# A feed-forward down projection by seven block products with tokens on partitions, in a two-layer fp32 trunk

## The chip, the cores and the metric

The kernel runs on one core of one Trainium2 chip. The metric is the time on the device of one execution, in microseconds (us); the median of several runs counts. The engines are TensorE (PE; its weight loads are PEld), VectorE (DVE), ScalarE (ACT), GpSimd (POOL) and SyncE (SP), which issues the DMA transfers of the kernel before.

## The reference

A trunk of two layers works on 512 tokens of 1024 features in float32. Layer 0 mixes the tokens with a gated recurrence (RG-LRU), layer 1 with stick-breaking attention over 16 heads. A root-mean-square norm stands ahead of each mixer and of each feed-forward part, and one at the very end. The feed-forward part, which the change is about, is

```python
def _swiglu(h, w_gate, w_up, w_down):
    g = h @ w_gate.astype(h.dtype)
    u = h @ w_up.astype(h.dtype)
    return (jax.nn.silu(g) * u) @ w_down.astype(h.dtype)
...
for each layer:
    x = x + mixer(_rmsnorm(x, g_mix))
    x = x + _swiglu(_rmsnorm(x, g_ffn), w_gate, w_up, w_down)
out = _rmsnorm(x, final_g)
```

with 2816 hidden features, so that `w_gate` and `w_up` are 1024 x 2816 and `w_down` is 2816 x 1024. (The last five lines are the reference's loop in short.)

## The kernel before

**Arithmetic.** Every large product is split to keep float32's accuracy: an operand is cast to fp32r on ACT (the high part, `wh` for weights, `hh`, `uh` for data), DVE or POOL subtracts that from the original (the low part `wl`, `hl`, `ul`), and PE runs high x high, high x low and low x high into one PSUM bank. One such triple is called mm3. Weights come as tiles of 128 x 1024, each loaded by one 512 KB transfer into a `raw` (or `b1`, `b3`) buffer. Such a tile is a *chunk*. `split_one` casts and subtracts it (L236, L237) two or three chunks ahead of its use.

**Layout.** The residual x is held transposed, as eight tiles `x0` to `x7` of 128 features x 512 tokens.

**Gate and up projections.** A feed-forward part runs in units u = 0 to 5 of 512 hidden features (256 for u = 5). Gate and up of a unit are computed by a one-level scheme of seven block products in place of eight (numbered 1, 5, 6, 3, 7, 2, 4), with tokens on partitions. Seven products need sums and differences of the blocks: those of the data are made once per layer (`ffn_in`), those of the weights per unit by DVE subtractions on 128 x 1024 tiles (`source`, L76), four per column of chunks, 88 in all. The results are combined into `r1`, `u2`, `b5`; SiLU is on ACT, and the products `u2` and `hx` are the hidden values with tokens on partitions.

**Down projection.** In unit u the hidden values of unit u-1 are transposed on PE (`turn`, L657, four banks), split into `hh` and `hl` (L660, L661), and multiplied by four chunks of `w_down` (`down_pair`): eight output tiles of 128 features x 512 tokens, each the sum of 4 k-tiles x 3 matmuls (L671 to L673), in the two banks `tb`; `add` (L676) adds each to its x. The last 256 features come after unit 5 in two chunks (`final`).

**The end.** In layer 0 each final add is followed by `norm_in`, which makes `uh` (L325), `ul` (L326) and the squares for attention's norm (L378, L380). In layer 1, `finish` scales x, transposes it on PE (L429), sums the squares on PE (L433), takes the root, and scales the rows out of PSUM (L454, L456) ahead of eight 256 KB stores (L457).

**Order.** Inside `ffn` only PE runs in the order of the program; DVE, ACT and POOL are ordered by a scheduler, with weight splits at high priority (`PRI`). All loads are on SP's queue; POOL does the low parts of the down chunks and additions of squares.

## Time and profile before

| what | value |
|---|---|
| median of 3 runs | 1148.85 us (1147.87 to 1149.36) |
| the profiled execution: its time | 1147.83 us |
| its span in the profile | 1146.0 us |
| feed-forward part, layer 0 / layer 1 | 166 to 512 / 785 to 1132 us |
| mean granted clock of PE | 0.995 |

The profile comes from one execution of its own; its span lies 1.8 us inside that execution's time. The busy time of an engine is read against the span; a wait is idle time of an engine ahead of an instruction, with the instruction that released it. Only what PE waits for, and what the end of the kernel takes, is on the way to the end. The windows view gives the same sums for a stretch; the timeline gives the start and the duration of single instructions, where a matmul's duration includes the depth of PE's pipeline, so that its price is the distance between starts.

### The profile page before, as it was taken

The numbers are of one execution on the slowest core, as the hardware profiler recorded it, in microseconds if no ns is written. First come the engines' busy times: TensorE is split into PE (matmuls) and PEld (weight loads), VectorE is DVE, ScalarE is ACT, GpSimd is POOL, SyncE is SP. The second block draws the span as 40 slices with busy tenths as digits, with TensorE's granted clock in tenths as the row PEclk, the third lists the DMA queues.
The fourth block names the chain that finished last, engine by engine and source line by source line (L and its number), as shares of the span: only waits on it lengthen the run. The fifth ranks groups of instructions, "written<-read, shape, count | busy, mean of one in ns | idle before, by whom it ended". The sixth has DMA issues, their size and how long they took to land.

```text
span 1146.0 us, 14365 instructions
## 1 busy us (share of the span) xinstructions
PE 1121.6 (98%) x5395; PEld 932.7 (81%) x5395; DVE 814.6 (71%) x1071; ACT 649.8 (57%) x969; POOL 295.1 (26%) x162
## 2 busy tenths in 40 slices
PE   9999999999999999999999999899999999999997
PEld 6887788788888888988888888778788888888896
DVE  7878889867574757473388888778967576675654
ACT  6598576634353444353489998767553534353443
POOL 2451333020111111262045345313011110211230
PEclk9999999999999999999999999999999999999999
DMA  7222234232423222122334234133433232322102
GB/s 244 89 90 89 98 105 171 95 110 76 142 74 129 73 92 92 55 92 92 111 97 125 82 86 110 37 99 122 147 110 110 73 114 80 121 86 99 58 35 74
DMA packets 36149, 114.23 MB, mean 100 GB/s; under 512 B 4592, under 2 KB 5616, under 8 KB 36080
## 3 DMA queue, kind: packets, MB, share of 16 engines
q1 hardware_dynamic: 36080, 113.32, 30.2%
q8 instruction: 42, 0.69, 0.2%
q14 instruction: 27, 0.22, 0.1%
HBM read 102.81 MB, written 2.10 MB: 92 GB/s over the span
## 4 chain that ended last, share of the span: by engine, by line
PE 74%; DVE 10%; ACT 4%; DMA 1%; issue 1%; POOL 0%; SPq 0%; DVEq 0%; POOLq 0%; ACTq 0%
PE bank L650 10%; PE bank L651 10%; PE bank L652 10%; PE bank L671 7%; PE bank L673 7%; PE bank L672 7%; PE bank L270 5%; PE bank L272 5%; PE bank L271 5%; DVE wl L237 4%; PE bank L974 3%; PE bank L657 2%; PE bank L1000 1%; DVE tt L76 1%; ACT wh L236 1%
## 5 line engine op out<-in xcount | busy, mean ns | idle before, releaser
L237 POOL TENSOR_TENSOR wl<-raw,wh 128x1024 fp32r<-128x1024 f32 (+1 forms) x74 | 178.5, 2412 | 641.9 <-ACT wh L236 638.0
L236 ACT CAST wh<-raw 128x1024 fp32r<-128x1024 f32 (+1 forms) x154 | 155.9, 1016 | 185.4 <-PE bank L652 88.1
L650 PE MATMUL bank<-wh,ow 128*128 128x512 f32 (+1 forms) x480 | 180.2, 375 | 3.8 <-DVE st L389 3.8
L651 PE MATMUL bank<-wl,ow 128*128 128x512 f32 (+1 forms) x480 | 178.9, 373 | 0.0
L652 PE MATMUL bank<-wh,ow 128*128 128x512 f32 (+1 forms) x480 | 178.8, 372 | 0.0
L236 ACT CAST wh<-tt 128x1024 fp32r<-128x1024 f32 x66 | 69.4, 1052 | 111.0 <-PE bank L672 55.1
L237 DVE TENSOR_TENSOR wl<-raw,wh 128x1024 fp32r<-128x1024 f32 (+1 forms) x80 | 97.9, 1227 | 45.4 <-ACT wh L236 44.4
L671 PE MATMUL bank<-hh,wh 128*128 128x512 f32 (+1 forms) x324 | 125.4, 387 | 0.0
L672 PE MATMUL bank<-hl,wh 128*128 128x512 f32 (+1 forms) x324 | 125.3, 387 | 0.0
L673 PE MATMUL bank<-hh,wl 128*128 128x512 f32 (+1 forms) x324 | 125.2, 387 | 0.0
L676 DVE TENSOR_TENSOR x<-x,bank 128x512 f32<-128x512 f32 x87 | 59.6, 685 | 85.1 <-PE bank L673 84.2
L650 PEld LDWEIGHTS bank<-wh,ow 128*128 128x128 f32 x480 | 90.8, 189 | 20.0 <-issue 2.7
L237 DVE TENSOR_TENSOR wl<-tt,wh 128x1024 fp32r<-128x1024 f32 x66 | 80.6, 1222 | 36.3 <-ACT wh L236 36.0
L270 PE MATMUL bank<-uh,wh 128*128 128x512 f32 x256 | 102.4, 400 | 1.7 <-ACT wh L236 1.1
L652 PEld LDWEIGHTS bank<-wh,ow 128*128 128x128 f32 x480 | 90.8, 189 | 15.8
L651 PEld LDWEIGHTS bank<-wl,ow 128*128 128x128 f32 x480 | 90.9, 189 | 15.4
L272 PE MATMUL bank<-uh,wl 128*128 128x512 f32 x256 | 100.2, 392 | 1.0 <-DVE wl L237 1.0
L271 PE MATMUL bank<-ul,wh 128*128 128x512 f32 x256 | 99.7, 390 | 0.3 <-DVE ul L326 0.3
L237 DVE TENSOR_TENSOR wl<-b,wh 128x1024 fp32r<-128x1024 f32 x44 | 54.8, 1246 | 51.8 <-ACT wh L236 51.6
L236 ACT CAST wh<-b 128x1024 fp32r<-128x1024 f32 x44 | 46.3, 1053 | 62.1 <-PE bank L652 26.7
L673 PEld LDWEIGHTS bank<-hh,wl 128*128 128x128 f32 x324 | 60.9, 188 | 12.4
L671 PEld LDWEIGHTS bank<-hh,wh 128*128 128x128 f32 x324 | 60.9, 188 | 12.1
(220 smaller groups left out, 2421.2 us busy)
## 6 DMA issues: line engine op xcount, KB each, us to landing
raw<-w_gu SPq DMA_DIRECT2D x44, 512.0 KB, 3.5
b<-w_gu SPq DMA_DIRECT2D x44, 512.0 KB, 4.0
raw<-w_dn SPq DMA_DIRECT2D x44, 512.0 KB, 3.5
raw<-w_qk SPq DMA_DIRECT2D x16, 512.0 KB, 3.5
raw<-w_in SPq DMA_DIRECT2D x14, 512.0 KB, 3.6
raw<-w_ao SPq DMA_DIRECT2D x8, 512.0 KB, 4.0
raw<-w_v SPq DMA_DIRECT2D x8, 512.0 KB, 3.5
qh<-qx SPq DMA_DIRECT2D x32, 128.0 KB, 2.4
```

What stands on the lines that cost most here:

```text
L236: self.nc.scalar.copy(wh[:, c], raw[:, c])
L237: self.wl_engine(i).tensor_tensor(wl[:, c], raw[:, c], wh[:, c].bitcast(F32), ALU.subtract)
L270: mm(out, lhsT=wh, rhs=xh, start=first, stop=False)
L271: mm(out, lhsT=wh, rhs=xl, start=False, stop=False)
L272: mm(out, lhsT=wl, rhs=xh, start=False, stop=last)
L650: mm(out[j][:, :w], lhsT=oh[:, ts(j)], rhs=wh[:, ws], start=st, stop=False, skip_group_check=True)
L651: mm(out[j][:, :w], lhsT=oh[:, ts(j)], rhs=wl[:, ws], start=False, stop=False, skip_group_check=True)
L652: mm(out[j][:, :w], lhsT=ol[:, ts(j)], rhs=wh[:, ws], start=False, stop=en, skip_group_check=True)
L671: mm(out, lhsT=w[0][:, ws], rhs=h[:, cs], start=st, stop=False, skip_group_check=True)
L672: mm(out, lhsT=w[0][:, ws], rhs=lw[:, cs], start=False, stop=False, skip_group_check=True)
L673: mm(out, lhsT=w[1][:, ws], rhs=h[:, cs], start=False, stop=en, skip_group_check=True)
L676: nc.vector.tensor_tensor(self.x[m], self.x[m], bank, ALU.add)
```

## The change

**Down projection.** The hidden values and `w_down` are now cut into 2 x 2 blocks as well. `dproduct` runs the seven block products d1 to d7 of a unit, 12 matmuls each, with *tokens on partitions*: results are added to `y`, four tiles of 128 tokens x 1024 features. The stationary operands are sums of transposed blocks of hidden values: t0 and t1 (`turn`) transpose the features 0, 2 and 1, 3 into the two banks `tb`, and `operands` makes the high and low parts `ha`, `hb`, `ht` from them (an ACT copy of one bank, four DVE sums of half tiles, then splits on ACT and DVE). t1 also copies `b5` out of the gate bank.

**Weight sums.** The sums of gate and up weights are made by *accumulating DMAs* on POOL's queue (`plus`): a piece of `w_gu` is added in memory to a buffer (`bu`, `bv`) that held an earlier piece, one chunk after the split that last read it (`soon`). In units 0, 1 and 5 ("direct") product 6's sum stays on DVE. There are 78 such transfers of 512 KB. The sums of `w_down` blocks are four POOL subtractions per unit (`DownPiece.after`), three of them behind d1's split. POOL also makes the low parts of the pieces d4, d5 and the second halves of products 2 and 7; DVE makes the others.

**x and y.** In layer 1, unit 0 transposes x into `y` (`turned`, steps x0 to x3, 32 transposes); in layer 0, y starts from the first block products, and at the end it is transposed back and added to x (`back`, 32 transposes). In layer 1 the last norm works on the rows of y (`finish`): per row tile two adds, two squares on ACT that also sum, a few 1-column operations, two scalings by the root and the gain, two stores.

**Order.** Inside `ffn`, ACT, DVE and POOL now stand in the order of the program as well. The steps of a unit are in strings (`order`). `plan` cuts the chunks in the same sequence. Splits run 4 chunks ahead and loads 9, x lies in the constant pool, slot pools have other sizes, `rsB` shares memory with `acc`.

The instructions change as follows: PE matmuls of 512 columns 4263 to 4161, of 256 columns 532 to 496, of 128 columns 408 to 440; DVE 1073 to 1245, ACT 971 to 1070, POOL 167 to 273.

Three places show how the program moves. First DVE in unit 3 of layer 0, around the down projection's operands. Before (`tt`, `b3`, `raw` are weight sums and their sources, `hl` the low hidden values, `wl` low weights):

```order
L237 TENSOR_TENSOR wl99_3124<-tt254_3121,wh99_3123 128x1024
L661 TENSOR_TENSOR hl0_96_3092<-bank6_76,hh0_96_3091 128x512
L661 TENSOR_TENSOR hl1_96_3100<-bank7_77,hh1_96_3099 128x512
L76 TENSOR_TENSOR tt254_3121<-b3_250_3037,tt254_3121 128x1024
L237 TENSOR_TENSOR wl101_3177<-tt253_3103,wh101_3176 128x1024
L661 TENSOR_TENSOR hl2_98_3148<-bank6_76,hh2_98_3147 128x512
L661 TENSOR_TENSOR hl3_98_3156<-bank7_77,hh3_98_3155 128x512
L76 TENSOR_TENSOR tt253_3103<-raw257_3231,tt253_3103 128x1024
```

After, from d1's split on (`t242` is the ACT copy in `operands`, `t243` and `t244` its sums):

```order
L295 TENSOR_TENSOR wl90_2803<-raw232_2662,wh90_2802 128x1024
L682 TENSOR_TENSOR t243_2832<-t242_2831,bank7_77 128x256
L681 TENSOR_TENSOR t244_2833<-t242_2831,bank6_76 128x256
L681 TENSOR_TENSOR t243_2832<-t243_2832,t242_2831 128x256
L681 TENSOR_TENSOR t244_2833<-bank7_77,t243_2832 128x256
L681 TENSOR_TENSOR hbl_1510<-bank7_77,hbh_1509 128x512
L681 TENSOR_TENSOR hal_1508<-t242_2831,hah_1507 128x256
L681 TENSOR_TENSOR htl_1512<-t243_2832,hth_1511 128x512
L681 TENSOR_TENSOR htl_1512<-t244_2833,hth_1511 128x512
L295 TENSOR_TENSOR wl91_2851<-bv_233_2683,wh91_2850 128x1024
L295 TENSOR_TENSOR wl492_2868<-bv_234_2702,wh492_2867 128x1024
L295 TENSOR_TENSOR wl93_2887<-raw235_2726,wh93_2886 128x1024
```

The weight sums are gone from DVE there; eight operations on hidden values stand in one block, and three splits follow them.

Second, POOL at the same place. Before, it holds only the low parts of down chunks:

```order
L237 TENSOR_TENSOR wl95_3016<-raw243_2873,wh95_3015 128x1024
L237 TENSOR_TENSOR wl4100_3160<-raw248_2995,wh4100_3159 128x1024
L237 TENSOR_TENSOR wl105_3266<-raw255_3127,wh105_3265 128x1024
L237 TENSOR_TENSOR wl4108_3334<-raw256_3199,wh4108_3333 128x1024
L237 TENSOR_TENSOR wl113_3446<-raw259_3305,wh113_3445 128x1024
```

After (`raw232` is block 11 of the unit's down weights, `raw235` block 21, `d12` and `d22` the other two, `dt` a sum of them):

```order
L152 TENSOR_TENSOR raw232_2662<-d12_236_2744,raw232_2662 128x1024
L152 TENSOR_TENSOR dt_241_2806<-d22_237_2746,raw232_2662 128x1024
L152 TENSOR_TENSOR d12_236_2744<-d22_237_2746,d12_236_2744 128x1024
L90 DMA bv_233_2683<-w_gu 128x1024
L90 DMA bv_234_2702<-w_gu 128x1024
L152 TENSOR_TENSOR dt_241_2806<-raw235_2726,dt_241_2806 128x1024
L295 TENSOR_TENSOR wl496_2940<-bv_234_2702,wh496_2939 128x1024
L295 TENSOR_TENSOR wl97_2958<-raw232_2662,wh97_2957 128x1024
```

Three subtractions stand ahead of the two transfers that add into `bv` for product 7, and a fourth behind them.

Third, DVE at the end of layer 0. Before:

```order
L676 TENSOR_TENSOR x0_1_78<-x0_1_78,bank3_73 128x512
L676 TENSOR_TENSOR x1_2_79<-x1_2_79,bank4_74 128x512
L326 SCALAR_TENSOR_TENSOR ul_286_3920<-x0_1_78,par_86,uh_285_3919 128x512
L676 TENSOR_TENSOR x2_3_80<-x2_3_80,bank5_75 128x512
L326 SCALAR_TENSOR_TENSOR ul_288_3932<-x1_2_79,par_86,uh_287_3931 128x512
L676 TENSOR_TENSOR x3_4_81<-x3_4_81,bank2_72 128x512
L326 SCALAR_TENSOR_TENSOR ul_291_3946<-x2_3_80,par_86,uh_290_3945 128x512
```

After, from the add of block 5 on:

```order
L682 TENSOR_TENSOR y1_1504<-y1_1504,bank3_73 128x512
L682 TENSOR_TENSOR x0_78<-x0_78,bank6_76 128x512
L393 SCALAR_TENSOR_TENSOR ul_298_4119<-x0_78,par_86,uh_297_4118 128x512
L682 TENSOR_TENSOR x1_79<-x1_79,bank7_77 128x512
L393 SCALAR_TENSOR_TENSOR ul_300_4129<-x1_79,par_86,uh_299_4128 128x512
L682 TENSOR_TENSOR x2_80<-x2_80,bank0_70 128x512
L295 TENSOR_TENSOR wl144_4268<-raw289_3925,wh144_4267 128x1024
L393 SCALAR_TENSOR_TENSOR ul_303_4141<-x2_80,par_86,uh_302_4140 128x512
L682 TENSOR_TENSOR x3_81<-x3_81,bank1_71 128x512
L393 SCALAR_TENSOR_TENSOR ul_306_4153<-x3_81,par_86,uh_305_4152 128x512
L682 TENSOR_TENSOR y2_1505<-y2_1505,bank4_74 128x512
L682 TENSOR_TENSOR y3_1506<-y3_1506,bank5_75 128x512
```

An add and the `ul` of the same x now follow each other, and the adds of the last two blocks into y2 and y3 stand behind the fourth `ul`.

The core of the diff (the methods of `ffn` are shown as they are now):

```diff
--- before
+++ after
-NS1 = 43
-NS2 = 30
+NS1 = 28
+NS2 = 37
...
+        self.direct = u in (0, 1, NU)
+        if u == 0:
+            order = "g1 g3 g5 g2 g6 g7 g4"
+        elif u == 1:
+            order = "g1 g5 g6 d1 g3 d2 d6 g7 d5 d7 g4 d3 d4 g2"
+        elif u < NU:
+            order = "g5 g1 g6 d1 g3 d2 d6 g7 d5 d7 g4 d3 d4 g2"
+        else:
+            order = "g5 g1 g6 d1 g3 d2 d6 d5 g7 d7 g4 g2 d4 d3"
+        self.pieces = []
+        for n in order.split():
+            q = int(n[1])
+            self.pieces += [Piece(self, q, c) for c in range(self.np)] if n[0] == "g" else [DownPiece(self, q)]
...
+    LOADS = {1: ("raw", 0), 2: ("raw", 2), 5: ("bu", 0), 3: ("bv", 3)}
+    HOME = {1: 1, 2: 2, 5: 5, 6: 5, 4: 5, 3: 3, 7: 3}
+    NEXT = {5: 3, 6: 2, 3: 1}
...
+    def plus(self, n):
+        kern = self.unit.kern
+        t = self.source()
+        kern.soon(lambda: kern.nc.gpsimd.dma_start(t, self.part(n), accum_op=ALU.add))
...
+    def sums(self):
+        un, kern = self.unit, self.unit.kern
+        if self.q == 6 and un.direct:
+            kern.nc.vector.tensor_tensor(self.source(), self.source(), un.b[3, self.c], ALU.add)
+
+    def after(self):
+        un, kern, q = self.unit, self.unit.kern, self.q
+        kern.done.add((un, q, self.c))
+        if q == 3:
+            if not un.direct or (un, 6, self.c) in kern.done:
+                self.plus(1)
+        elif q == 5:
+            if not un.direct:
+                self.plus(3)
+        elif q == 6:
+            self.plus(2)
+            if un.direct and (un, 3, self.c) in kern.done:
+                Piece(un, 3, self.c).plus(1)
...
+class DownPiece(Piece):
+    def __init__(self, unit, q):
+        self.unit, self.q, self.c = unit, q, 0
+        self.pool = q in (5, 4)
...
+    def after(self):
+        kern, d = self.unit.kern, self.unit.d
+        sub = lambda o, x, y: kern.soon(lambda: kern.nc.gpsimd.tensor_tensor(d[o], d[x], d[y], ALU.subtract))
+        if self.q == 1:
+            d["t"] = self.buf("dt", kern.fp, 1)
+            sub("11", "12", "11")
+            sub("t", "22", "11")
+            sub("12", "22", "12")
+        elif self.q == 6:
+            sub("t", "21", "t")
...
+    def soon(self, f):
+        self.later.append((self.used, f))
...
-            return self.nc.vector if isinstance(self.chunks[i], Piece) else self.nc.gpsimd
+            e = self.chunks[i]
+            return self.nc.gpsimd if isinstance(e, Piece) and e.pool else self.nc.vector
...
-        ahead = ahead or (self.AHEAD_SPLIT if self.ring4 is None else 3)
-        more = self.AHEAD_LOAD if self.ring4 is None else 8
-        while self.loaded < min(n, i + more):
-            self.load_one()
+        while self.later and self.later[0][0] <= i:
+            self.later.popleft()[1]()
+        ffn = self.ring4 is not None and i < self.ffn_end
+        ahead = ahead or (4 if ffn else self.AHEAD_SPLIT)
+        more = 9 if ffn else self.AHEAD_LOAD
...
+    def finish(self, y, ys, g):
+        nc, st = self.nc, self.st
+        for t, (yt, pair) in enumerate(zip(ys, y)):
+            s0, s1, v, r = (st[:, 4 * t + i:4 * t + i + 1] for i in range(4))
+            sq = self.tmp()
+            hs = [slice(0, S), slice(S, D)]
+            for h, b, s in zip(hs, pair, (s0, s1)):
+                nc.vector.tensor_tensor(yt[:, h], yt[:, h], b, ALU.add)
+                nc.scalar.activation(sq, yt[:, h], AF.Square, accum_out=s)
+            nc.vector.tensor_tensor(s0, s0, s1, ALU.add)
+            nc.vector.tensor_scalar(v, s0, 1.0 / D, EPS, ALU.mult, ALU.add)
+            nc.scalar.activation(s1, v, AF.Sqrt)
+            nc.vector.reciprocal(r, s1)
+            nc.vector.scalar_tensor_tensor(s0, v, -0.5, r, ALU.mult, ALU.mult)
+            nc.vector.tensor_tensor(s0, s0, r, ALU.mult)
+            nc.vector.scalar_tensor_tensor(r, s0, 1.5, r, ALU.add, ALU.mult)
+            for h in hs:
+                nc.vector.scalar_tensor_tensor(yt[:, h], yt[:, h], r, g[:, h], ALU.mult, ALU.mult)
+                nc.sync.dma_start(self.out[t, :, h], yt[:, h])
...
+        with tc.tile_pool(name=f"ffn{l}", bufs=1) as self.fp, \
+                tc.manual_schedule(engines={E.PE, E.Activation, E.DVE, E.Pool}):
...
+            def operands(p):
+                bx, by = tb
+                cx, ta, tc_ = (self.tmp() for _ in range(3))
+                nc.scalar.copy(cx, bx)
+                add(ta[:, T0], cx[:, T1], by[:, T1])
+                sub(tc_[:, T0], cx[:, T0], bx[:, T1])
+                sub(ta[:, T1], ta[:, T0], cx[:, T0])
+                sub(tc_[:, T1], by[:, T0], ta[:, T1])
+                split([t[:, p] for t in hb], by)
+                split([t[:, p] for t in ha], cx[:, T0])
+                for i, t in enumerate((ta, tc_)):
+                    split([o[:, p, 2 * i:2 * i + 2].rearrange("p a b -> p (a b)") for o in ht], t)
...
+            DOWN = {1: (db, True, 0, 0), 2: (tb, True, 0, 0), 6: (db, False, 0, 1), 5: (tb, True, 1, 1),
+                    7: (db, False, 1, 1), 3: (tb, False, 0, 1), 4: (db, False, 1, 0)}
+
+            def dproduct(q):
+                wh, wl = self.chunk()
+                banks, first, a, d = DOWN[q]
+                for i in range(2):
+                    for p in range(2):
+                        mm3(banks[i], *stat(q, p, i), wh[:, ts(p, S)], wl[:, ts(p, S)], first and p == 0, p == 1)
+                for i in range(2):
+                    t = 2 * a + i
+                    o = y[t][:, ts(d, S)]
+                    if gnext and (t, d) not in started:
+                        started.add((t, d))
+                        nc.scalar.copy(o, banks[i])
+                    else:
+                        add(o, o, banks[i])
...
+                def t0():
+                    turn((0, 2), tb)
+                    operands(0)
+
+                def t1():
+                    turn((1, 3), tb)
+                    b5_copy()
+                    operands(1)
+
+                def tn():
+                    turn((0, 1), A)
+                    for p in range(2):
+                        split([t[:, p] for t in hb], A[p])
...
+                    order = "g1 x0 g3 x1 g5 g2 g6 stats g7 gate1 x2 g4 x3"
+                elif u == 1:
+                    order = "g1 t0 g5 t1 g6 d1 g3 d2 d6 g7 d5 d7 g4 d3 d4 g2"
+                elif u < NU:
+                    order = "g5 t0 g1 t1 g6 d1 g3 d2 d6 g7 d5 d7 g4 d3 d4 g2"
+                else:
+                    order = "g5 t0 g1 t1 g6 d1 g3 d2 d6 d5 g7 d7 g4 g2 d4 tn d3"
...
+            def last(t, h, b):
+                for p in range(2):
+                    mm3(b, *(o[:, p, ts(t)] for o in hb), *(o[:, ts(h, S)] for o in ws[p]), p == 0, p == 1)
+
+            if gnext:
+                def back(h, banks):
+                    for i, b in enumerate(banks):
+                        m = 4 * h + i
+                        for t in range(NT):
+                            nc.tensor.transpose(b[:, ts(t)], y[t][:, ts(m)], self.ident)
+                        add(self.x[m], self.x[m], b)
+                        self.norm_in(m, gnext)
+
+                for n in range(8):
+                    h, t = divmod(n, NT)
+                    last(t, h, free[n])
+                    o = y[t][:, ts(h, S)]
+                    add(o, o, free[n])
+                    if n == 5:
+                        back(0, free[:4])
+                back(1, free[4:])
+            else:
+                nc.scalar.activation(self.st[:, 0:1], self.ones[:, 0:1], AF.Sqrt)
+                g = self.raw_buf()
+                nc.sync.dma_start(g, self.a["g_row"])
+                for t in range(NT):
+                    for h in range(2):
+                        last(t, h, free[2 * t + h])
+                self.finish([free[2 * t:2 * t + 2] for t in range(NT)], y, g)
```

418 lines of the change are left out of this document (165 added, 253 removed).

## The prediction

> **What bounds the kernel now.** The page's first lines come first, then busy time by stage, then what TensorE (PE) waits for.
>
> ```profile
> span 1146.0 us, 14365 instructions
> PE 1121.6 (98%) x5395; PEld 932.7 (81%) x5395; DVE 814.6 (71%) x1071; ACT 649.8 (57%) x969; POOL 295.1 (26%) x162
> ```
>
> The windows view gives us, then busy time of PE, PEld, DVE, ACT and POOL, then granted clock and DMA share, for the feed-forward part of layer 0, that of layer 1, and the end of the kernel.
>
> ```profile
> 166.00:512.00 346.00, 343.05 (x1638) 287.50 (x1637) 239.92 (x266) 161.96 (x206) 76.53 (x30) 1.00 0.31 104
> 785.00:1132.00 347.00, 343.37 (x1649) 288.32 (x1648) 236.49 (x264) 160.37 (x203) 65.28 (x24) 1.00 0.28 94
> 1132.00:1146.00 14.00, 6.27 (x58) 6.03 (x56) 5.27 (x14) 4.04 (x8) 0.00 (x0) 0.83 0.41 151
> ```
>
> PE is busy 343 of 346 us in both feed-forward parts at the full granted clock. The list of PE's waits (total, times, longest, in us) is headed by
>
> ```profile
> PE bank L650 <- DVE st L389: 3.8, 2, 2.3
> PE bank L919 <- DVE awl L989: 2.9, 3, 2.3
> PE bank L657 <- DVE x L676: 2.8, 8, 0.3
> ```
>
> so no wait there exceeds 2.3 us. Fewer matmuls are worth their full time, and any new lateness of another engine is paid in full. Only in the last 14.0 us is PE not the bound.
>
> **PE's work.** Prices are start-to-start distances in the timeline (start, duration): seventeen matmuls of 512 columns, twenty-four of 256, and the 24 transposes of the old last norm in one row.
>
> ```profile
> 300.16 0.39 PE L672 MATMUL bank<-hl,wh 128*128 128x512 f32 x1
> ...
> 303.79 0.39 PE L673 MATMUL bank<-hh,wl 128*128 128x512 f32 x1
> ```
>
> ```profile
> 1123.57 0.28 PE L671 MATMUL bank<-hh,wh 128*128 128x256 f32 x1
> ...
> 1126.32 0.28 PE L673 MATMUL bank<-hh,wl 128*128 128x256 f32 x1
> ```
>
> ```profile
> 1135.45 2.82 PE L429 MATMUL bank<-ident,xg 128*128 128x128 f32 x24
> ```
>
> That is 3.63/16 = 0.227, 2.75/23 = 0.120 and (2.82 - 0.27)/23 = 0.111 us. A full unit's down projection falls from 8 x 4 x 3 = 96 matmuls to 7 x 12 = 84: 12 x 5 units x 2 layers = 120 fewer. The old code ran 18 of layer 1's matmuls as 36 halves of 256 columns; they come back as 18 whole ones. Net 102 x 0.227 = -23.1 and 36 x 0.120 = -4.3. Layer 0 gains 32 transposes (y back to x), layer 1 gains 32 ahead (x to rows, in unit 0): 64 x 0.111 = +7.1. Sum **-20.3 us**; the 32 transposes taken out of the old end belong to the next term.
>
> **The end of the kernel.** Real matmuls end here, and dependent four-column operations on DVE follow each other at 0.2 us:
>
> ```profile
> 1131.86 0.28 PE L673 MATMUL bank<-h,wl 128*128 128x256 f32 x1
> ...
> 1135.63 0.26 ACT L385 ACTIVATE st<-bank,eps 128x4 f32<-128x4 f32 x1 [1.84 <-PE bank L433]
> ...
> 1136.21 0.16 DVE L388 SCALAR_TENSOR_TENSOR st<-st 128x4 f32<-128x4 f32 x1
> 1136.40 0.16 DVE L389 TENSOR_TENSOR st<-st 128x4 f32<-128x4 f32 x1
> ```
>
> The transfers of the stretch 1136 to 1146, in GB/s for each quarter of a us, fade out near 1144.2, 1.8 before the end:
>
> ```profile
> GB/s 0 0 0 0 0 0 0 0 33 90 369 385 393 360 393 377 393 369 377 393 369 401 369 361 393 393 377 393 393 377 393 254 41 8 0 0 0 0 0 0
> ```
>
> Durations (busy us, then mean ns) from the groups, for this and the next parts:
>
> ```profile
> L237 POOL TENSOR_TENSOR wl<-raw,wh 128x1024 fp32r<-128x1024 f32 x70 | 174.6, 2495 | 634.1 <-ACT wh L236 630.3 <-DVE qy L893 3.7
> L676 DVE TENSOR_TENSOR x<-x,bank 128x512 f32<-128x512 f32 x87 | 59.6, 685 | 85.1 <-PE bank L673 84.2
> L237 DVE TENSOR_TENSOR wl<-tt,wh 128x1024 fp32r<-128x1024 f32 x66 | 80.6, 1222 | 36.3 <-ACT wh L236 36.0
> L76 DVE TENSOR_TENSOR tt<-raw,tt 128x1024 f32<-128x1024 f32 x22 | 26.8, 1217 | 0.2
> L334 DVE TENSOR_TENSOR t<-t,t 128x256 f32<-128x256 f32 x16 | 6.7, 420 | 0.2
> L530 DVE SCALAR_TENSOR_TENSOR sv<-t,sv 128x512 f32<-128x512 f32 x8 | 5.2, 689 | 5.8 <-ACT t L529 5.8
> L236 ACT CAST wh<-tt 128x1024 fp32r<-128x1024 f32 x66 | 69.4, 1052 | 111.0 <-PE bank L672 55.1 <-PE bank L652 34.0 <-issue 13.7
> L660 ACT CAST hh<-bank 128x512 fp32r<-128x512 f32 x40 | 22.2, 588 | 0.7
> L378 ACT ACTIVATE t<-x 128x512 f32<-128x512 f32 x33 | 20.3, 624 | 3.5 <-DVE x L676 3.2
> L325 ACT ACTIVATE uh<-x,par 128x512 fp32r<-128x512 f32 x16 | 11.5, 722 | 9.4 <-DVE x L676 7.0 <-DMA x<-xT 2.1
> outT<-raw SPq DMA_DIRECT2D x8, 256.0 KB, 3.2
> ```
>
> In the new end DVE stands in program order, so each row tile's chain runs by itself: two adds 1.37, the second square on ACT 0.62, two small operations 0.4, ACT's root and back 0.4 (0.26 and the way), four small ones 0.8, two scalings 1.38: about 5.0 us against PE's 12 x 0.227 = 2.7 per tile. The first add can start 1.4 us after the last block starts; with the first tile's later half at 2.7 the four tiles end near 22.7, PE at 10.9. Behind them come one store (3.2 with eight in the queue; I take 2.8) and those 1.8. So 22.7 + 4.6 - 10.9 = 16.4 us beyond PE in place of 14.0: **+2.4** (from 0, if squares overlap the next tile's adds, to +5).
>
> **The end of layer 0.** The new order of DVE puts the whole of back(0), four times add, uh on ACT, ul, with one weight split between, ahead of the adds that free y2 and y3; the old one let them interleave, and PE did not wait there. From the end of block 5: the add of y1 0.9, four times (0.685 + 0.72 + 0.69) = 8.4, the split 1.2, two adds 1.4: 11.9 us. PE meanwhile has 16 transposes (1.8) and 12 matmuls (2.7), and its next transposes need y2: 7.2 us of waiting. Then the first matmuls of the v projection write the banks that x6 and x7 are added from. x6's add ends 0.3 + 2 x 2.1 + 0.7 = 5.2 later, with 1.6 of transposes to cover it; x7's comes 2.1 behind it, with three matmuls (0.7) between: 3.6 + 1.4. Sum **+12.2** (7 if only the first wait is real; 16 if POOL's three additions of squares, beside these, each hold DVE back).
>
> **Inside the units.** These rows show what I use most. DVE and POOL exclude each other when both work from SBUF:
>
> ```profile
> 254.03 2.40 POOL L237 TENSOR_TENSOR wl<-raw,wh 128x1024 fp32r<-128x1024 f32 x1 [8.48 <-ACT wh L236]
> ```
>
> ```profile
> 254.37 3.15 DVE L76 TENSOR_TENSOR tt<-b,raw 128x1024 f32<-128x1024 f32 x1
> ```
>
> DVE's 1.22 us operation lasted 3.15, past POOL's end. And POOL starves while DVE runs such operations back to back:
>
> ```profile
> 176.89 9.76 POOL L380 TENSOR_TENSOR acc<-acc,t 128x512 f32<-128x512 f32 x1 [7.85 <-ACT t L378]
> ```
>
> ```profile
> 176.79 1.22 DVE L237 TENSOR_TENSOR wl<-tt,wh 128x1024 fp32r<-128x1024 f32 x1
> ...
> 184.27 1.22 DVE L237 TENSOR_TENSOR wl<-b,wh 128x1024 fp32r<-128x1024 f32 x1
> 185.41 0.68 DVE L697 TENSOR_TENSOR r<-r,bank 128x512 f32<-128x512 f32 x1
> 186.00 1.73 DVE L237 TENSOR_TENSOR wl<-b,wh 128x1024 fp32r<-128x1024 f32 x1
> ```
>
> It got its turn only when DVE read PSUM at 185.41. Now a unit 2 to 4, zero at its first matmul: products 5 and 1 with t0 end at 11.8, t1 at 12.7, product 6 at 18.1, d1 at 20.8, product 3 at 26.3, d2 at 29.0, d6 at 31.7, then product 7. POOL's first subtraction starts behind the split of the down piece, 12.9 to 15.3. ACT's three copies after t1 (3 x 0.59) let DVE start the operands at 14.5: two of 0.42 from PSUM, one from SBUF to 15.75. There DVE reads PSUM twice, and POOL's second subtraction takes 15.75 to 18.15. DVE's hal waits for it, to 18.55; the two htl end at 19.9, the next three splits (3.6 us) at 23.4; the first is needed at 21.05, just met. POOL's third subtraction runs only when DVE turns to PSUM: 23.4 to 25.8. Only then does POOL's queue reach the accumulating transfer for product 7, whose cast (1.05) and split (1.22) must be through by 31.9. The stall is X - 3.8, X being issue to landing of that transfer. No row shows an accumulating transfer; plain ones of the same size:
>
> ```profile
> raw<-w_gu SPq DMA_DIRECT2D x44, 512.0 KB, 3.5
> b<-w_gu SPq DMA_DIRECT2D x44, 512.0 KB, 4.0
> ```
>
> I take X = 4.0, the nearest, with bounds 3.5 and 7.0 (a second pass at 3.5). That is +0.2 in each of three units. Unit 1 still sums product 6 on DVE, 2 x 1.22 ahead of ha for d1: +2.5, and X - 3.65. In unit 5 a gate or up product has one chunk of 24 x 0.120 = 2.9 us. Gate 1 of unit 4 (add, two ACT gates, two scalings, about 3.6) is late for t0 by 0.75; operands(0) must leave the banks (0.2 + 0.59 + 4 x 0.42 + 0.68, with its waits 4.2) before t1, +1.3; and d1 comes 2.9 after t1 where hal needs the two htl of operands(0), the copies, four of 0.42, hbl and one subtraction of POOL, 7.3 in all: +4.4. Sum 6.45. A layer: 3 x 0.2 + 2.5 + 0.35 + 6.45 = 9.9; both **+19.8**.
>
> The Trainium skill, "DMA: Bandwidth & Descriptors", section "Anatomy of one DMA", fits 2.0 us + bytes/436e3 for a transfer queued by GpSimd: an estimate of 3.2 us for 512 KB, and "Collectives: The Full Stack" says that an add needs two source reads, which makes it an estimated 4.4. By that the sum would be 3.2 us higher (eight units' stalls x 0.4); no run here shows it yet.
>
> **Costed at nothing.** The 88 sums taken off DVE (88 x 1.22 = 107 us) never held PE, and DVE is at 71%. 78 transfers more move 39 MB beside the present traffic: at 0.31 of the DMA engines' time the share becomes about 0.42, 0.53 if an accumulation costs double, so others should hardly feel it; if they do it shows as X. Pools, aliases, hold and load distance change no instruction's length; a buffer freed late would show as a late load, at most one chunk, 2.7 us, per place.
>
> **The sum.** -20.3 + 2.4 + 12.2 + 19.8 = +14.1 on the profiled execution's 1147.83 is 1161.9. The median of the runs, 1148.85, lies 1.0 above that execution: **1162.9 us**. About 0.2% (2.3 us) is what a measurement of this kernel can tell from no change.
>
> **The rivals.** *A, the other engines keep pace.* If DVE, freed of 107 us, is early enough that neither the units nor the end of layer 0 wait, -20.3 + 2.4 remain: 1131. For it: DVE at 71%, and waits of 2.3 at most before. Against: the written order at the end of layer 0 leaves DVE no choice. *A', only the end of layer 0 waits:* -5.7, 1143. It decides if ACT's and POOL's parts run ahead of my times, above all if the subtractions find free stretches earlier; my 2.9 us between t1 and d1 in unit 5 speaks against. *B, accumulating transfers are slow.* Each us of X over 4.0 costs one us in units 1 to 4 of both layers, 8 in all; the point is X = 3.8, and at X = 7 it is +24: 1187. For: such a transfer reads its target as well. Against: the queue has 70% free. *C, the port goes to whoever asks first.* Then POOL's third subtraction slips in after hal, 18.55 to 20.95, and the htl and split for product 3 end at 23.5 in place of 21.1: 2.4 in place of 0.2 in six units, +13.2: 1176. The row at 176.89 speaks against it: POOL asked for 8 us.
>
> The Trainium skill, "SBUF — State Buffer", section "SBUF: two separate sides", calls the pair of ports an exclusive lock held for the whole instruction by whichever starts first. The trace agrees with the lock (3.15 for 1.22), not with a turn for POOL after each DVE instruction.
>
> **Chances and range.** Forecast 0.36, A 0.16, A' 0.24, B 0.13, C 0.11. A and A' keep 0.40 between them, since my unit timeline chains a dozen durations, and operands ready 4 us earlier would undo most of the 19.8. The forecast alone holds 1154 to 1171 (X at 3.5 to 4.5, the end of layer 0 at 7 to 16). The range takes in A at 1131 with 2 us below it, A', C, and B up to X = 6: 1129 to 1180, leaving out half of B and the lower part of A. Faster by over 0.2%: A and most of A', 0.38; within: the edges of A' and of the forecast, 0.04; slower: 0.58.
>
> **What would show it.** PE instructions of 512 columns 102 fewer at unchanged clock; a wait of PE on y2's add and one on x6's near the end of layer 0, some 12 us; PE waits of about 4 before d1 of unit 5 in both layers, of under 1 before product 7 in units 2 to 4; POOL's third subtraction stretched or late behind DVE's splits; 16 us from last matmul to end. The prediction is wrong if PE's waits in the two feed-forward parts sum to less than 15 us (A, A'), if the transfers land after more than 5 us (B), or if PE waits before product 3 (C).

## The result, and the profile after

The changed kernel takes **1200.22 us** (median of 4 runs, 1198.91 to 1207.4) against 1148.53 for the kernel before beside it: 51.7 us more, a ratio of 1.046 with a 95% interval of 1.042 to 1.050. The direction was forecast, the size was not: 1162.9 lies 37 us below, outside the range.

The page's head after the change:

```profile
span 1198.4 us, 14804 instructions
PE 1118.7 (93%) x5265; PEld 917.2 (77%) x5265; DVE 921.5 (77%) x1243; ACT 703.2 (59%) x1076; POOL 416.9 (35%) x268
```

PE works 2.9 us less and sits idle more. DVE has become busier, not freer: it runs 172 operations more, and an operation that is held at the SBUF port counts as busy for all that time (the two htl of unit 2 below: 3.50 for 1.29). The windows view, for layer 0's feed-forward part up to the v projection, for layer 1's, and from the last two chunks on (columns as before: busy PE, PEld, DVE, ACT, POOL, then granted clock and DMA share):

```profile
167.50:535.00 367.50, 339.82 (x1593) 280.00 (x1591) 283.17 (x333) 185.22 (x250) 134.05 (x79) 0.98 0.60 152
818.00:1173.00 355.00, 333.70 (x1557) 275.90 (x1557) 271.94 (x325) 180.56 (x242) 129.09 (x77) 0.97 0.55 139
1173.00:1198.40 25.40, 11.12 (x48) 8.88 (x48) 15.06 (x41) 6.60 (x20) 0.00 (x0) 0.80 0.22 83
```

Three things stand out against the kernel before: over 20 us of idle PE in each part, a granted clock below 1, and POOL at nearly twice its load. The list of PE's waits now begins

```profile
PE bank L691 <- DVE wl L295: 19.0, 9, 2.4
PE bank L690 <- ACT u L793: 8.1, 2, 4.7
PE bank L690 <- ACT hah L686: 6.0, 4, 1.9
PE bank L697 <- DVE hbl L681: 3.8, 3, 1.7
PE bank L465 <- DVE r L682: 3.3, 2, 2.3
```

where the longest total before was 3.8. And the transfers, first by queue (q0 is POOL's: packets, MB, share of 16 engines' span), then from issue to landing:

```profile
q1 hardware_dynamic: 36224, 113.84, 28.5%
q0 software_dynamic: 11232, 40.90, 19.5%
```

```profile
bu<-w_gu POOLq DMA_DIRECT2D x56, 512.0 KB, 6.9
bv<-w_gu POOLq DMA_DIRECT2D x22, 512.0 KB, 7.0
```

X, for which 4.0 was taken, is 7.0, the upper bound.

To place the 52.4 us of span, take the distance from each matmul's start to the next, less the row's price (0.227, 0.120, 0.111). Excesses over 0.4 us are waits. Of the small ones about half lie in stretches of halved clock; the rest, at full clock, is some 0.1 us behind each wait (308.52 to 308.86 below is 0.34 in place of 0.227) and waits of under 0.4. PE's work is the count of matmuls at these prices (the median distance of 512 columns is 0.227 in both traces). By place, both layers together, less the same in the kernel before (its waits were 0.5 at each of eight transpositions, 1.7 and 2.4 in unit 0):

| term | forecast | measured |
|---|---|---|
| PE's work | -20.3 | -20.6 |
| unit 0 | 0 | +8.5 |
| unit 1 | +5.7 | +12.4 |
| units 2 to 4 | +1.2 | +11.3 |
| unit 5 | +12.9 | +11.3 |
| end of layer 0 | +12.2 | +4.9 |
| start of layer 1's part | 0 | +2.4 |
| end of the kernel | +2.4 | +0.6 |
| small excesses at half clock | 0 | +11.1 |
| small excesses at full clock | 0 | +9.6 |
| rest | 0 | +0.9 |
| sum | +14.1 | +52.4 |

The table says where the time lies. It does not say what the kernel gains when one of these waits is removed: e3 and e6 below show waits that come back at the next place.

**Units 2 to 4.** PE's one wait is before the low weights of product 3, in the second matmul of that product:

```profile
305.93 0.39 PE L690 MATMUL bank<-wh,ow 128*128 128x512 f32 x1
308.52 0.50 PE L691 MATMUL bank<-wl,ow 128*128 128x512 f32 x1 [2.21 <-DVE wl L295]
```

POOL's three subtractions at that place, and its transfers, in unit 2:

```profile
298.64 2.43 POOL L152 TENSOR_TENSOR raw<-d,raw 128x1024 f32<-128x1024 f32 x1
301.14 2.49 POOL L152 TENSOR_TENSOR dt<-d,raw 128x1024 f32<-128x1024 f32 x1
303.60 2.58 POOL L152 TENSOR_TENSOR d<-d,d 128x1024 f32<-128x1024 f32 x1
308.83 0.88 POOL L90 DMA_DIRECT2D bv<-w_gu  x1 [2.65 <-DVE wl L295]
```

and DVE beside them (hal and htl are the low parts of the operands):

```profile
303.08 0.84 DVE L681 TENSOR_TENSOR hal<-t,hah 128x256 fp32r<-128x256 f32 x1
303.84 3.50 DVE L681 TENSOR_TENSOR htl<-t,hth 128x512 fp32r<-128x512 f32 x2
307.26 2.35 DVE L295 TENSOR_TENSOR wl<-bv,wh 128x1024 fp32r<-128x1024 f32 x2
```

The third subtraction is recorded from 303.60, when hal is still running, and the two htl (1.29 for both in undisturbed places) last 3.50, to just past its end and their own time. That is rival C almost to the tenth: with the unit's zero at 284.9 (5.44 ahead of t0's first transpose at 290.38) it runs from 18.7 where C said 18.55, and PE waits 2.4. The first transfer for product 7 is issued 23.9 after zero, not 25.8, and its 7 us just fit: no wait there.

**Unit 0.** ACT in written order stands at a cast that waits for an accumulating transfer; the copies that free product 6's bank are queued behind it:

```profile
193.70 1.05 ACT L294 CAST wh<-bv 128x1024 fp32r<-128x1024 f32 x1 [6.04 <-DMA bv<-w_gu]
199.91 1.04 ACT L294 CAST wh<-bv 128x1024 fp32r<-128x1024 f32 x1 [5.15 <-DMA bv<-w_gu]
200.86 1.04 ACT L294 CAST wh<-bu 128x1024 fp32r<-128x1024 f32 x1
201.80 1.07 ACT L793 COPY u<-bank 128x512 f32<-128x512 f32 x2
```

**Unit 1.** The wait before d1 was forecast; product 3's is that of units 2 to 4. DVE's third sum for the operands takes 2.08 in place of 0.42 beside POOL's first subtraction:

```profile
236.15 2.08 DVE L681 TENSOR_TENSOR t<-t,t 128x256 f32<-128x256 f32 x1
```

```profile
235.52 2.42 POOL L152 TENSOR_TENSOR raw<-d,raw 128x1024 f32<-128x1024 f32 x1
```

**The clock.** In the windows view by single microseconds (granted clock third from the end) PE idles from 198 on and restarts at 202.4:

```profile
198.00:199.00 1.00, 0.00 (x0) 0.00 (x0) 0.00 (x0) 0.00 (x0) 0.00 (x0) 0.58 0.99 360
202.00:203.00 1.00, 0.56 (x1) 0.50 (x2) 1.00 (x2) 0.98 (x3) 0.00 (x0) 0.50 0.00 0
206.00:207.00 1.00, 1.00 (x4) 0.79 (x3) 0.90 (x5) 0.00 (x0) 0.00 (x0) 0.50 0.76 311
209.00:210.00 1.00, 1.00 (x6) 0.82 (x5) 0.92 (x1) 0.98 (x2) 0.23 (x1) 1.00 0.88 307
```

For six microseconds of work the clock is at a half, 3 us lost behind a wait of 4.8. After the single wait of 2.4 us at 306 it stayed at 1.00. That is no rule: the same wait in unit 3 of layer 1, at 1020.6, is followed by a halved stretch, and unit 5 of layer 0 has five waits, 8 us in all, at full clock:

```profile
472.00:492.00 20.00, 12.80 (x88) 10.72 (x87) 18.12 (x24) 10.99 (x22) 9.09 (x5) 1.00 0.31 54
1024.00:1028.00 4.00, 4.00 (x12) 3.15 (x11) 3.74 (x5) 0.00 (x0) 1.41 (x3) 0.57 0.76 128
```

### The profile page after: what moved, and what is told of

It reads as the page before. It is cut to its first block, busy times and chain, and to the rows that moved or that the text cites. A ratio compares the mean times of both kernels' runs of the same rounds, so it can differ in the third digit from the quotient of the medians.

```text
span 1198.4 us, 14804 instructions
## 1 busy us (share of the span) xinstructions
PE 1118.7 (93%) x5265; PEld 917.2 (77%) x5265; DVE 921.5 (77%) x1243; ACT 703.2 (59%) x1076; POOL 416.9 (35%) x268
## 3 DMA queue, kind: packets, MB, share of 16 engines
q0 software_dynamic: 11232, 40.90, 19.5%
## 5 line engine op out<-in xcount | busy, mean ns | idle before, releaser
L295 POOL TENSOR_TENSOR wl<-raw,wh 128x1024 fp32r<-128x1024 f32 (+1 forms) x44 | 108.6, 2468 | 143.5 <-ACT wh L294 143.5
L90 POOL DMA_DIRECT2D bu<-w_gu x56 | 49.2, 883 | 298.8 <-DVE wl L295 223.8
L294 ACT CAST wh<-bu 128x1024 fp32r<-128x1024 f32 x66 | 69.5, 1053 | 82.7 <-PE bank L692 38.1
L295 DVE TENSOR_TENSOR wl<-bu,wh 128x1024 fp32r<-128x1024 f32 x66 | 85.4, 1294 | 31.5 <-ACT wh L294 30.4
L682 DVE TENSOR_TENSOR y<-y,bank 128x512 f32<-128x512 f32 x140 | 89.9, 678 | 11.0 <-PE bank L692 10.7
L294 ACT CAST wh<-bv 128x1024 fp32r<-128x1024 f32 x44 | 45.4, 1050 | 87.6 <-DMA bv<-w_gu 84.7
L295 DVE TENSOR_TENSOR wl<-bv,wh 128x1024 fp32r<-128x1024 f32 x36 | 44.0, 1240 | 45.3 <-ACT wh L294 45.1
L1026 POOL TENSOR_TENSOR spl<-t,sph 128x512 fp32r<-128x512 f32 (+1 forms) x32 | 36.3, 1158 | 85.5 <-DVE sph L1025 79.8
L691 PE MATMUL bank<-wl,hth 128*128 128x512 f32 x160 | 62.4, 390 | 0.2 <-POOL wl L295 0.2
L690 PE MATMUL bank<-wh,hth 128*128 128x512 f32 x160 | 62.5, 390 | 0.0
```

Of the source, the lines that this page charges most:

```text
L90: kern.soon(lambda: kern.nc.gpsimd.dma_start(t, self.part(n), accum_op=ALU.add))
L294: self.nc.scalar.copy(wh[:, c], raw[:, c])
L295: self.wl_engine(i).tensor_tensor(wl[:, c], raw[:, c], wh[:, c].bitcast(F32), ALU.subtract)
L682: add = lambda o, a, b: nc.vector.tensor_tensor(o, a, b, ALU.add)
L690: mm(out, lhsT=xh, rhs=wh, start=first, stop=False, skip_group_check=True)
L691: mm(out, lhsT=xh, rhs=wl, start=False, stop=False, skip_group_check=True)
```

## The experiments

Seventeen kernels, one execution timed of each, beside one of the kernel before (1147.9 to 1149.9). Like waits are followed by a halved stretch in one place and not in another, at about 1.7 us a time (half of the shortest stretch, 3.4); gaps of under 4 us between runs are not read here. Edits are on the kernel after the change (1200) where nothing else is said.

**e1: the third subtraction later.**

```diff
             sub("t", "22", "11")
-            sub("12", "22", "12")
         elif self.q == 6:
             sub("t", "21", "t")
+            sub("12", "22", "12")
```

> POOL's third subtraction for the down weights moves from d1's split to behind the fourth, four chunks later. Port theory (POOL's third subtraction slips in between DVE's hal and htl and so delays product 3's low weights): the eight waits before product 3 in units 1 to 4 of both layers (2.4 to 2.6 us each, 19.5 in all) go, and with them some of the half clock after unit 1's; time about 1178. Transfer theory (everything is late because an accumulating transfer takes 7 us): product 3 is fed by a plain load, the wait moves to another place, 1195 to 1203.

Measured 1178.42, 21.8 less. All eight waits before product 3 are gone from the distances, and in unit 2 the htl take their plain time:

```profile
300.09 1.28 DVE L681 TENSOR_TENSOR htl<-t,hth 128x512 fp32r<-128x512 f32 x2
301.29 2.35 DVE L295 TENSOR_TENSOR wl<-bv,wh 128x1024 fp32r<-128x1024 f32 x2
```

Some 18 of the 22 us are gained at these eight places. One line of order, and the port, cost them. In unit 5 new waits of 1.9 and 1.0 us appear, for low weights that POOL makes.

**e2: plain transfers.**

```diff
-        kern.soon(lambda: kern.nc.gpsimd.dma_start(t, self.part(n), accum_op=ALU.add))
+        kern.soon(lambda: kern.nc.gpsimd.dma_start(t, self.part(n)))
```

> The 78 transfers on POOL's queue overwrite their buffer in place of adding to it; the sums of gate and up weights that they made are left out, all else is the same. Transfer theory: they land in about 4 us in place of 7, and most of the 52 us goes: about 1160. Port theory: the waits before product 3 stay at 2.4 us; only unit 0's wait for ACT's copies, which stand behind a cast that waits for a transfer, goes (6 us, with 5 of half clock behind it, in layer 0; 4 and 3 in layer 1): about 1184.

This kernel leaves the sums out. Measured 1177.98; landing 4.6 and 4.4 us in place of 6.9 and 7.0. The waits before product 3 stayed in units 2 to 4 (2.3 each); unit 0's wait for the copies fell to 0.8 and 0.9, without its half clock. Adding has a price of its own, but not where rival B put it.

**e3: unit 0's casts behind the copies.** In unit 0 the splits run 3 and 2 chunks ahead in place of 4.

```diff
-                        wh, wl = self.chunk()
+                        wh, wl = self.chunk({2: (3, 3), 6: (3, 2)}.get(q, (None, None))[c] if u == 0 else None)
```

> In unit 0 the casts of product 7's second half are written behind ACT's copies out of product 6's bank, not ahead of them; transfers and sums are unchanged. Queue theory (the copies wait only because they stand behind a cast that waits for a transfer): unit 0's wait of 4.8 us (3.6 in layer 1) falls to under 2, the half clock behind it goes, 5 to 7 us per layer in all: about 1188. Transfer theory: product 7 itself waits for the same transfer, 1197 to 1201.

Measured 1200.58. The copies' wait went, but product 7 then waited for the transfer itself (1.4 and 1.0 us in layer 0, 2.6 and 1.0 in layer 1); the distances show 7.8 us less waiting in all and 10.8 more at half clock, most of it at other places (219, 369, 489 us). The queue theory alone fails: the transfer is late there, whoever waits for it. That the time is unchanged to within 0.4 us is chance, since the added half clock lies elsewhere.

**e5: the scheduler's order.**

```diff
-                tc.manual_schedule(engines={E.PE, E.Activation, E.DVE, E.Pool}):
+                tc.manual_schedule(engines={E.PE}):
```

> Inside the feed-forward parts DVE, ACT and POOL are ordered by the scheduler as in the kernel before, PE alone in program order; the work is the same. If the written order makes the waits: 1150 to 1175. If data dependences and the times of transfers and subtractions make them: 1190 to 1210, with the same waits before product 3 and in unit 0.

Measured 1166.47, 33.8 less with the same work. The waits before product 3 and for unit 0's copies are gone; others are there:

```profile
PE bank L692 <- DVE hal L681: 10.8, 8, 1.4
PE bank L697 <- DVE hbl L681: 10.2, 5, 3.1
```

Of the 33.8, 5.0 us lie at the end of the kernel: from the start of the last matmul to the end it takes 9.7 in place of 14.7, here and in the four other kernels in the scheduler's order. DVE there makes the last row tile's adds (1155.55) ahead of the second's scalings (1156.33).

**e4: back behind the last blocks.**

```diff
-                    if n == 5:
+                    if n == 7:
                         back(0, free[:4])
```

> At the end of layer 0 the back transposes of x0 to x3 are written behind the last two blocks, so that y2's and y3's adds stand ahead of the four add, uh, ul chains on DVE. If those late adds hold PE, its waits there (1.3, 0.7, 1.5 us and about 3 us of half clock) go: 1194 to 1196. If the chains themselves are what the v projection waits for, PE now waits earlier for the same chains, and loses the blocks that covered them: 1199 to 1203.

Measured 1200.22: nothing in the sum. PE's waits at the end of layer 0 (4.9 before) became a series of four of about 0.6 and one of 1.4 (4.1 with smaller ones). Matched matmul by matmul, e4 gains 1.7 us of waits there and 1.7 more because the halved stretch at 549.7 does not come; later places, unit 0 of layer 1 first (a wait of 5.4 in place of 3.7), take both back. So the adds of y2 and y3 held PE for 1.7 us at most; what is left, the v projection waits for in the four chains.

**e6: filler in unit 0.**

```diff
                     self.norm_rs1(False)
+                    for i in range(16):
+                        mm(tb[1], lhsT=self.held[0][:, :P], rhs=self.held[0], start=True, stop=True,
+                           skip_group_check=True)
```

> Sixteen matmuls of 512 columns into an unused bank are added in unit 0 of both layers, where PE waits 4.8 and 3.6 us for ACT's copies; nothing else changes. Clock theory (PE's clock halves after a long wait and stays so for some us): the clock stays at 1.0 there, and some 5 us in layer 0 and 3 in layer 1 are saved while the waits' length is filled, not shortened: 1192 to 1196. If the half clock is no cost of the wait: 1200 or above, by up to 1 us in each layer.

Measured 1194.5, inside the first range: PE does 7 us of useless work and the kernel gains 5.7. The clock there stays at 1.00:

```profile
202.00:203.00 1.00, 1.00 (x6) 0.82 (x5) 1.00 (x3) 0.99 (x3) 0.00 (x0) 1.00 0.96 373
206.00:207.00 1.00, 0.41 (x2) 0.00 (x0) 1.00 (x2) 0.99 (x3) 0.00 (x0) 1.00 0.00 0
```

But the 5.7 us do not come from there, and the hit is luck. Matched matmul by matmul, e6 is 1.5 us ahead from the kernel's first 34 us on, where nothing was changed; 4.4 ahead at 208, at the end of the halved stretch; and 1.5 again at 249, in unit 1's product 3. Product 4 now waits 1.6 for product 7's adds, and t1 waits 2.2 in place of 0.6. In layer 1 the lead goes from 5.2 (856) to 7.3 (860) and back to 5.0 (901). The lead that lasts arises elsewhere, 1.5 us each, for instance, where the halved stretches at 549.7 and 819.4 do not come. So in unit 0 the half clock is no more than time that the next waits would have taken.

**e7 and e8: four places mended.** The second subtraction goes to `self.q == 2`, the third behind the fourth; in unit 0, `plus(2)` moves from product 6 to product 7; gate banks are `2 * (i ^ l)`; unit 4 ends "g4 g2 d3 d4". e7 keeps the written order, e8 takes the scheduler's.

> Written order kept on all engines, with four changes: POOL's second and third down subtractions stand behind the transfers into bv; in unit 0 the transfers for product 7 go ahead of those for product 4; layer 1's first gate bank is not the one that attention's last tile is read from; unit 4 runs gate 1 two block products earlier. Port and queue theory: from 1178 (third subtraction alone) minus 5 for hal in unit 1, 10 for unit 0 with its half clock, 4 at the start of layer 1's part, 5 for t0 of unit 5: about 1154. Transfer theory: no gain beyond unit 0's: 1168 to 1178.

> The same four changes, with DVE, ACT and POOL ordered by the scheduler. Port and queue theory: from the scheduler's 1166 minus 1.5 us times eight before hal, about 5 in unit 5, 4 at the start of layer 1's part: 1143 to 1150. If the scheduler has already found those gains: 1162 to 1168.

Measured 1199.08 and 1166.68: both readings of e7 fail; e8 lies inside its second. In e7 unit 0's wait fell to 2.0 and 0.7, and the start of layer 1's part waits no more, but product 7 now waits 1.1 to 2.1 in eight units, since its low weights on POOL queue behind the moved subtractions (line numbers are e7's own):

```profile
308.97 3.34 POOL L157 TENSOR_TENSOR dt<-raw,dt 128x1024 f32<-128x1024 f32 x1 [3.50 <-DVE wl L301]
312.26 2.41 POOL L157 TENSOR_TENSOR d<-d,d 128x1024 f32<-128x1024 f32 x1
314.62 2.38 POOL L301 TENSOR_TENSOR wl<-bv,wh 128x1024 fp32r<-128x1024 f32 x1
```

Unit 5 waits 3.3 at t1 in e7 and 6.4 in e8, with gate 1 of unit 4 moved.

**e9 and e10: fewer moves.** e9 is e1 with unit 0's transfers reordered and the other bank; e10 is e1 with the other bank and the scheduler's order.

> Written order kept; the third subtraction alone is moved as in e1, unit 0's transfers for product 7 go ahead of those for product 4, and layer 1 starts in a bank that attention no longer reads. If waits add up singly: 1178 minus 2.4 and 1.6 of half clock at the start of layer 1's part, minus 4 of wait and 3 to 5 of half clock in unit 0 of each layer: 1159 to 1166. If unit 0's transfers only move the wait (as e3's order did): 1172 to 1176.

> DVE, ACT and POOL ordered by the scheduler, third subtraction moved, other first bank in layer 1. The scheduled kernel's waits before hal (eight of 1.5 us) come from a POOL subtraction that holds the port; if it is the third one, they go: 1148 to 1153; if it is the first or second, they stay: 1160 to 1167.

Measured 1169.07, between the two readings, and 1167.58, at the edge of the second. In e9 unit 0's waits at and behind product 7 come to 2.0 (layer 0) and 1.5, and the start of layer 1's part waits no more. In e10 the eight waits before hal stay: it is not the third subtraction's place in the program, since the scheduler puts all three together again, beside the operands of DVE:

```profile
296.19 1.94 DVE L681 TENSOR_TENSOR t<-t,t 128x256 f32<-128x256 f32 x1
298.06 0.41 DVE L681 TENSOR_TENSOR hal<-t,hah 128x256 fp32r<-128x256 f32 x1
```

```profile
294.49 3.36 POOL L152 TENSOR_TENSOR d<-d,d 128x1024 f32<-128x1024 f32 x1
```

**e11: e1 with e2's plain transfers.**

> Third subtraction moved and the 78 transfers overwriting in place of adding, the sums that they made left out. If the port (22 us) and the accumulating transfers (22 us) are separate causes, the gains add: 1154 to 1158. If they are one cause seen from two sides: 1170 to 1178.

Measured 1167.93, between the two readings: of 22 + 22 some 32 came. By the distances e1 takes 19 us of waits and 3 of small excesses, e2 13 and 9, both together 24 and 8. The eight waits before product 3 and unit 0's are separate; in units 1 and 5, and in the clock, each edit had taken some of what the other takes.

**e12: the subtractions on DVE.**

```diff
-        sub = lambda o, x, y: kern.soon(lambda: kern.nc.gpsimd.tensor_tensor(d[o], d[x], d[y], ALU.subtract))
+        sub = lambda o, x, y: kern.soon(lambda: kern.nc.vector.tensor_tensor(d[o], d[x], d[y], ALU.subtract))
```

> All four subtractions of down weights per unit run on DVE, at the same place of the written order, in place of POOL; 40 operations of 1.22 us more on DVE, 40 of 2.4 us fewer on POOL. Port theory: nothing holds DVE's operands any more, but they now stand behind three of DVE's own subtractions, 3.7 us in place of 7.2: the waits before product 3 go, those before d1 stay: 1178 to 1190. If the port has nothing to do with it, DVE's added work makes the operands later still: 1200 to 1215.

Measured 1202.21, in the second range, but not as either reading had it. The waits before d1 in unit 1 are gone, those before product 3 are there, 2.56 in units 2 to 4 and 3.9 in unit 1: in DVE's order the three subtractions stand between htl and the split of product 3.

```profile
303.85 1.29 DVE L681 TENSOR_TENSOR htl<-t,hth 128x512 fp32r<-128x512 f32 x2
305.06 1.22 DVE L152 TENSOR_TENSOR raw<-d,raw 128x1024 f32<-128x1024 f32 x1
...
308.59 2.35 DVE L295 TENSOR_TENSOR wl<-bv,wh 128x1024 fp32r<-128x1024 f32 x2
```

So the subtractions cost at this place on either engine; on POOL the port puts them into DVE's line just as the program does here. For the port itself the evidence is e1 with the stretched rows (3.50, 2.08), not this run.

**e13 and e14: all subtractions later.** e9 with the first two behind d2's split, the third behind product 7's low weights; e14 with the scheduler's order.

> As e9 (1169), with all four down subtractions of a unit behind the transfers into bv, the third of them behind POOL's low weights for product 7. If the first subtraction beside the operands makes what is left in units 1 and 5, the waits before d1 in unit 1 (2.6 us) and t1 in unit 5 (1.8 and 1.3) fall to about a half in both layers, with 1 to 3 of half clock: 1158 to 1163. If the operand chain itself is too long: 1167 to 1171.

> The same kernel with DVE, ACT and POOL ordered by the scheduler (1166 to 1168 so far). If a subtraction holds the port ahead of hal, the eight waits of 1.5 us go: 1150 to 1157. If the scheduler pulls the subtractions ahead again, since their inputs are there: 1164 to 1168.

Measured 1199.92 and 1163.27. In e13 product 3's waits are gone, and unit 1's before d1 too; but d6 and d7 now wait for their weights (1.0 and 1.8 us a unit): both its readings fail, by the same mechanism as e7. In e14 the waits before hal stay at 1.5, as its second reading had it. The port works both ways, as DVE shows at the end of unit 2 in e13, held through two operations of POOL:

```profile
332.56 5.65 DVE L822 SCALAR_TENSOR_TENSOR b<-b,nrs,t 128x512 f32<-128x512 f32 x1
```

```profile
332.58 2.73 POOL L302 TENSOR_TENSOR wl<-dt,wh 128x1024 fp32r<-128x1024 f32 x1
334.95 2.71 POOL L302 TENSOR_TENSOR wl<-raw,wh 128x1024 fp32r<-128x1024 f32 x1
```

**e15, e16, e17: taking the work away.** e15 drops the `sub` calls; e16 drops `accum_op` as well; e17 is e16 in the scheduler's order.

> The kernel after the change without the 40 subtractions of down weights (left out; the block products use the loaded blocks), transfers as they are. Port theory: the waits before product 3 go (20 us with their half clock), those before d1 in unit 1 and t1 in unit 5 shrink by about half: 1165 to 1175, below e1's 1178. If e1's gain came from some other effect of its order, and not from taking POOL off the port: 1178 to 1200.

> Subtractions left out and transfers overwriting (their sums left out), written order on all engines. If the accumulating transfers make what is left in unit 0: 1166 minus about 12: 1152 to 1157. If the written order of the operand chains makes it: 1162 to 1166.

> The same work, DVE, ACT and POOL ordered by the scheduler. With the waits for POOL and the transfers gone, only PE's smaller work and the waits of the operand chains at t0 and t1 remain: 1138 to 1148, below the kernel before. If the scheduled operand chains wait as the written ones do: 1150 to 1157.

All three leave sums out. Measured 1166.21, 1145.6 and 1133.53. e15 met its first expectation; e16 and e17 went below both readings of theirs: with POOL's line empty the additions were worth 21 us, not 12. The longest waits of e17 are ones that the kernel before has too, or stand at a part's start:

```profile
PE bank L998 <- DVE awl L1068: 2.9, 3, 2.3
PE bank L685 <- DVE x L1126: 2.3, 1, 2.3
```

So, in this sequence: 1200 minus 34 for the subtractions, minus 21 for the additions in transfers, minus 12 for the written order (5 of them at the kernel's end), is 1133.5, 16 us below the kernel before (1149.75 beside it). In another sequence the shares differ (e2: 22 for the additions alone; e11). PE's smaller work is a real gain; the 40 new subtractions and the 78 adding transfers together cost 55 us. The subtractions are work that the kernel before did not have, and no run makes the gate and up sums on DVE again. No kernel with all its work done came below the kernel before; the nearest is e14 at 1163.

## Why the prediction was wrong

1. *PE's work* held: -20.6, -20.3 forecast, at an unchanged distance of 0.227.
2. *The end of the kernel*: DVE's chain per row tile is 5.0 us as forecast (adds start at 1180.33 and 1185.34). The first row below is the last scaling, the span ends 3.0 us behind it; 4.6 were allowed for. +0.6 in place of +2.4. The written order itself costs 5.0 us there (e5), of which the forecast's lower end, 0, knew nothing.

```profile
1194.03 1.41 DVE L493 SCALAR_TENSOR_TENSOR y<-y,st,raw 128x512 f32<-128x512 f32 x2
```

3. *The end of layer 0* failed as a step, and on the favourable side. DVE's chain ran as worked out (y1's add at 530.49, y2's at 541.46, 11 us later). But PE's next work was not the back transposes: two of them stand at 534.78, the next 13 only at 542.79, and in between PE runs matmuls of the v projection on x0 to x3. The forecast took PE's order from the code; the order after scheduling, from which the document shows only DVE at that place, has the v projection pulled up. +4.9 of waits in place of +12.2, and some 2 of half clock; by e4 the adds account for 1.7 us of it at most.

```profile
534.78 0.38 PE L865 MATMUL bank<-ident,y 128*128 128x128 f32 x2
...
542.79 1.64 PE L865 MATMUL bank<-ident,y 128*128 128x128 f32 x13 [0.21 <-DVE y L682]
```

4. *Units 2 to 4*: the step "POOL's third subtraction runs only when DVE turns to PSUM" failed. It was taken from one row of before, where POOL seemed to starve for 8 us; here POOL came in after a single DVE operation. Rival C, at 0.11, was the case, with its place and its 2.4 us; e1 shows it (22 us, some 18 of them at the eight places), e12 that a subtraction anywhere between htl and the split costs as much. The rest of that unit's timeline was within 1 us.
5. *X* was 7.0, rival B's end, but not with B's effect: C's earlier issue hid it in units 2 to 4, and it came out in unit 0, which had been costed at nothing. The transfers into bv there land 7 and 10 us after their issue, behind those into bu; e2 and e3 show the transfer as cause, e16 that it is worth 21 us once POOL's line is free.
6. *Unit 1* was forecast at the right place (hal for d1: 2.5, measured 2.6 in each layer) and half its size: product 3's wait, 2.6 a layer, came on top, and in layer 0 2.1 us at t1 and product 6. Why DVE is late at d1 stays open: without the subtractions (e15) that wait is gone, though product 6's sums are still on DVE, but 2.7 us appear at t1 in layer 0 and 1.5 at product 6 in layer 1. *Unit 5* has the right sum, 11.3 against 12.9, by luck: d1 was to wait 4.4 in each layer and waited 2.1 and 0.6, t0 0.75 and waited 2.8 and 0.5, t1 1.3 and waited 1.9; 1.3 a layer, for ACT's copies of r, were not forecast.
7. *The clock* was no term at all: "at unchanged clock" stood among the signs. At half clock lie 11.1 us of the 38 that the forecast missed, as much as units 2 to 4 (10.1); the 9.6 us of small excesses at full clock had no term either. What the clock costs at the end is not shown: e6 kept it full in unit 0 and gained nothing there.
8. *The start of layer 1's part* (2.4) was overlooked: its first gate bank is the one that attention's last tile is read from, a clash that the old rotation of banks avoided; e9 ends it.

So the steps that failed are POOL's turn at the port (units 2 to 4, and product 3 of unit 1), the transfers that unit 0 waits for, costed at nothing, and the small delays behind waits, costed at nothing. Rival C's mechanism and B's slow transfer, named as alternatives, happened together; the range let each stand alone.

## What to carry to other kernels

On a kernel whose PE is 98% busy, work given to a helper engine has to land where nobody queues: here new sums went to POOL and old ones to DMAs, came back to DVE through the shared port and to ACT through its queue, and cost 55 us where PE saved 21. Allow for the clock behind new waits (11 us here), but do not take a filled or moved wait for a gain before the next wait has been read (e3, e6). Before moving an operation out of one wait's way, look what its own queue carries behind it: e7 and e13 moved more and gained nothing, where e1 moved one operation and gained 22.

## What the runs showed of the hardware

- The clock was halved after some waits and not after others: during a wait of 4.9 us behind one of 1.1 (197), after 2.6 us behind 2.0 and 0.6 (242), after a single 2.4 (1020.6); not after five other waits of 2.4 and 2.5 in units 2 to 4, nor in unit 5 of layer 0 (8 us of waits in 20). The halved stretches in the feed-forward parts last 3.4 us, or 6.8 and 10.2, two and three times that. The Trainium skill, "TensorE: Matmul & The Clock Gate", section "Part 1: The HAM clock gate (the "warmup" mystery)", describes a free-running activity window of about 3.4 us, with half rate after an idle one. The trace agrees with the length, and a free-running window would let like waits end differently; it does not agree that a whole window must be idle, since PE had waited only 2.4 us at 1020.6.
- An accumulating transfer keeps the DMA engines busy twice as long: q0's 40.90 MB took 19.5% of the span (1198.4 us) with the adds and 10.0% of e2's (1176.3) without. The Trainium skill, "Collectives: The Full Stack", section "The bandwidth ceiling: the fold count and why AG ≠ RS ≠ AR", puts the halved rate of a reduce between cores down to the add's two source reads; no run here separates reads from writes.
- Who gets the port next is not settled: POOL came in after one DVE operation at 303.60, DVE waited for two of POOL's in e13, and in the kernel before POOL's operation at 176.89 lasted 9.76 us beside a row of DVE's.
